# Three weight chunk halves get slots of their own in SBUF, and one goes back to the ring

## The chip, the cores and the metric

The kernel runs on one core of one Trainium2 chip. The metric is the device time of one execution in microseconds; before the change it is 531.22 us, the median of three runs (530.62 to 531.57). The names of the engines: PE is TensorE (PEld its weight loads), DVE is VectorE, ACT is ScalarE, POOL is GpSimd, and SP is the queue from which the loads are issued.

## The reference

One layer of a decoder trunk on 256 positions and 1024 features. Cut to what matters, the products that the change touches are these:

```python
h = rms_norm(x, norm_mix_g)
u_conv, q, kc, vc, ks, vs, kw, vw, g_nsa_heads, g_conv, g_attn = split(h @ w_in)
conv_out = silu(layer_norm(depthwise_conv(a * sigmoid(gt)) + b)) @ conv_pw_w
nsa_out  = nsa_attention(q, kc, vc, ks, vs, kw, vw, g_nsa_heads)
y = sigmoid(g_conv) * conv_out + sigmoid(g_attn) * nsa_out
x = x + y @ w_out
x = x + cross_attention(rms_norm(x, norm_x_g), mem)
x = x + swiglu(rms_norm(x, norm_ffn_g))
out = rms_norm(x, final_norm_g)
```

q is 1024 columns of `w_in`, `g_attn` 1024 more, and `conv_pw_w` is 1024 by 1024; everything is float32.

## The kernel before

**Chunks.** All weights are cut into chunks of 256 output columns, in the order in which they are used: k0 to k3 (cross-attention keys), u0 to u7 (the convolution's input), kc, vc, q0 to q3, ks, kw, vs, vw, ga0 to ga3 (the attention gate), gc0 to gc3 (the convolution's gate), pw0 to pw3, wo0 to wo3, xq0 to xq3, v0 to v3 (placed among the scores), xo0 to xo3, and the feed-forward chunks f. A chunk comes in two loads of 512 KB, each with four of the eight blocks of 128 input features. The two are called halves of a chunk here: q3_0 is the first half of the fourth q chunk, q3_1 its second.

**High and low.** To multiply float32 numbers with the faster type (fp32r), each operand is split into a high part (rounded by a copy) and a low part (the rest). `split` (L193) makes both for a chunk half: ACT copies the high part (L205), and a subtraction gives the low one (L208), on POOL for the chunks u3 to ga3 and on DVE for the others. Each product is then three: high by high, high weights by low activations, low weights by high activations. `rows` (L286) issues these for a chunk half, 24 matmuls (L297) of 128x128 weights on 256 moving columns: 16 with the high part of the weights, then 8 with the low part. In the profile a row `ps_q<-hh,q_0h` is such a matmul: the sum of a q chunk, moving operand hh (the high part of h; hl is the low one), weights the high part of a first half. The number of the chunk is left out in these names, but not that of the half.

**Where the halves lie.** Usually a high part takes one of five buffers of a ring (tag `whi`), and a low part one of five of a second ring (`wlo`). A chunk half named in `set_apart` (L217) lies elsewhere: with two tags, its high part begins 64 elements into the large slot of the first tag, and its low part 112 elements into the slot of the second. The large slots, L0 to L14, hold 8 KB for each partition and are shared by tiles that live at different times; LL is twice as large. The slots that the change names hold, one after the other:

- L9: `hf` (h as float32, read last by the gate logits, `g_ps`, L710), later `stacked`.
- L10 and L14: `kdh` and `kdl`, the keys of the scores, read until the last score product; later `yh` and `yl`.
- L11 and L13: in L13 `zins`, the input of the compression MLP; later `sga` and `sgc`, the two gates.

In the kernel's layout the start of a moving operand stands 448 bytes, modulo 512, behind the start of the weights that follow when those lie in a ring. For a high part set apart it is 256, and for a low part set apart 64.

**What sets the order.** Each engine works through its own queue in order, and the order of each queue is set when the kernel is built, by a scheduler that takes what becomes ready first by its own estimate. TensorE's order from kc on is held besides by `in_line`. A tile of a pool can be written when the last reader of the tile that lay there before is done, so where a half lies also sets what its copy has to wait for, and so where the copy stands in ACT's, DVE's or POOL's queue. The products run in the order of the chunks, with score products, transposes and outputs of the attention put between the chunks from ga0 on; pw0 to pw3 (L1040), wo and xq0 follow each other without anything between.

Of the kernel before, what the change touches and what calls it, by code (L numbers as in the profile page):

```python
# [118 lines left out]
def tile_hybrid_block(  # L119
# [97 lines left out]
    def set_apart(name, tag, low=None):  # L217

        pair = []

        def hi():
            pair.append(sb.tile([P, 1024 + 64 if low else 2 * 1024 + 112], F32R, tag=tag, name=f"{name}h"))
            return pair[0][:, 0:1024 + 64]

        def lo():
            if low:
                return sb.tile([P, 1024 + 112], F32R, tag=low, name=f"{name}l")[:, 112:]
            return pair[0][:, 1024 + 112:]

        apart[name], aparts[name] = hi, lo  # L230
# [2 lines left out]
    set_apart("xq1_0", "LL")  # L233
    set_apart("xq2_0", "LL")
    set_apart("xo0_1", "LL")
    set_apart("ks_0", "L11", "L13")
    set_apart("f2_0", "L9", "L0")

    def behind(*marks):
# [1314 lines left out]
```

## The time and the profile before

| | |
|---|---|
| three timed runs | 530.62, 531.22, 531.57 us |
| profiled execution, its own time | 528.97 us |
| span of it | 527.2 us |
| TensorE busy | 520.1 us, 4319 instructions |
| DVE, ACT, POOL busy | 442.3, 368.4, 147.4 us |
| granted clock of TensorE, mean | 0.997 |

The profile covers the profiled execution, which has a time of its own beside its span; the timed runs were made without it. In a timeline a row stands for several like instructions: its start, how long they took together, the engine, the line, the operation, `out<-in`, the shapes, and their number. Matmuls overlap, so the time that one adds is read from the distance of two starts and not from its own duration. A grouped row ends with the busy time, the mean duration of one in ns, and the idle time before. A window's row gives its length and then the busy time of PE, PEld, DVE, ACT and POOL, each with a count, the granted clock, the share of the DMA engines and GB/s.

### The profile page before, as it was taken

To read this page: it belongs to the slowest core of one execution; us is meant where nothing else is said; L and a number is where in the kernel's file an instruction comes from. 1 tells how busy PE (TensorE), PEld (TensorE's weight loads), DVE (VectorE), ACT (ScalarE), POOL (GpSimd) and SP (SyncE) were. 2 spreads that over 40 slices of the span, in tenths; PEclk is the share of its full clock that TensorE was granted. 3 is DMA by queue.
4 is the path that set the end of the run, shared out by engine and by line. 5 is a ranking of instruction groups with operands and counts; after the bars stand their busy time and mean duration, and the time that the engine had idled before them with its cause. 6 is when DMAs were issued, how large, how long until landed. Compare 5 with 4: busy or idle time off the path is not lost.

```text
span 527.2 us, 11194 instructions
## 1 busy us (share of the span) xinstructions
PE 520.1 (99%) x4319; PEld 502.4 (95%) x4319; DVE 442.3 (84%) x861; ACT 368.4 (70%) x671; POOL 147.4 (28%) x105
## 2 busy tenths in 40 slices
PE   9999999999999999999999999999999999999995
PEld 8999999999899999999999999999999999988884
DVE  4887899999999999984969685688988786689996
ACT  5678784999967899789648675565665555557743
POOL 0019889999995000330004000310000000000002
PEclk9999999999999999999999999999999999999998
DMA  8947966544545436224667542368665665625402
GB/s 315 410 168 250 322 202 212 165 161 153 166 160 184 160 127 208 88 81 160 222 217 274 192 156 99 109 197 300 229 219 192 197 201 188 201 93 159 162 0 81
DMA packets 29445, 97.20 MB, mean 184 GB/s; under 512 B 3152, under 2 KB 5456, under 8 KB 29136
## 3 DMA queue, kind: packets, MB, share of 16 engines
q1 hardware_dynamic: 28816, 95.44, 53.9%
q10 hardware_dynamic: 576, 1.05, 0.5%
q8 instruction: 34, 0.56, 0.4%
q14 instruction: 19, 0.16, 0.1%
HBM read 95.23 MB, written 1.25 MB: 183 GB/s over the span
## 4 chain that ended last, share of the span: by engine, by line
PE 98%; DVE 1%; ACT 0%; issue 0%; ACTq 0%
PE ps_f L297 23%; PE ps_u L297 8%; PE fo L1313 6%; PE ps_v L297 4%; PE ps_gc L297 4%; PE ps_ga L297 4%; PE ps_q L297 4%; PE ps_xq L297 4%; PE ps_pw L297 4%; PE ps_wo L297 4%; PE fos L1313 4%; PE ps_k L297 3%; PE ps_xo L297 3%; PE ps_xo L1198 2%; PE o L920 1%; PE s L852 1%
## 5 line engine op out<-in xcount | busy, mean ns | idle before, releaser
L494 DVE SCALAR_TENSOR_TENSOR yp<-vt,ppt,yp 128x256 f32<-128x256 f32 x144 | 64.2, 485 | 6.3 <-ACT yp L486 4.6
L1382 POOL TENSOR_TENSOR x<-xs,gf 128x512 f32<-128x512 f32 x2 | 2.6, 1302 | 168.3 <-issue 168.3
L297 PE MATMUL ps_f<-g,f_1h 128*128 128x256 f32 x352 | 44.4, 277 | 0.0
L297 PE MATMUL ps_f<-g,f_0h 128*128 128x256 f32 x352 | 43.9, 277 | 0.0
L297 PEld LDWEIGHTS ps_f<-g,f_1h 128*128 128x128 f32 x352 | 41.9, 188 | 0.0
L297 PEld LDWEIGHTS ps_f<-g,f_0h 128*128 128x128 f32 x352 | 41.8, 188 | 0.0
L205 ACT ACTIVATE f_0h<-f 128x1024 fp32r<-128x1024 f32 x22 | 23.4, 1062 | 18.9 <-issue 15.5
L886 ACT ACTIVATE p<-p,mins 128x128 f32<-128x128 f32 (+1 forms) x64 | 28.3, 449 | 10.2 <-DVE mins L865 10.0
L208 DVE TENSOR_TENSOR f_1l<-f,f_1h 128x1024 fp32r<-128x1024 f32 x22 | 27.4, 1247 | 5.6 <-ACT f_1h L205 5.6
L208 DVE TENSOR_TENSOR f_0l<-f,f_0h 128x1024 fp32r<-128x1024 f32 x22 | 27.3, 1243 | 3.2 <-ACT oxh L346 2.2
L205 ACT ACTIVATE f_1h<-f 128x1024 fp32r<-128x1024 f32 x22 | 23.2, 1060 | 9.4 <-PE ps_f L297 7.9
L486 ACT ACTIVATE vw<-vt,ppt 128x256 f32<-128x256 f32 x60 | 26.6, 499 | 0.6 <-DVE yp L508 0.5
L1272 DVE TENSOR_TENSOR ab<-ps_f,rf 128x512 f32<-128x512 f32 x22 | 15.2, 689 | 11.6 <-PE ps_f L297 11.6
L297 PE MATMUL ps_f<-g,f_1l 128*128 128x256 f32 x176 | 23.6, 277 | 0.0
L297 PE MATMUL ps_f<-g,f_0l 128*128 128x256 f32 x176 | 23.6, 276 | 0.0
L208 POOL TENSOR_TENSOR u_0l<-u,u_0h 128x1024 fp32r<-128x1024 f32 x5 | 12.0, 2404 | 37.5 <-ACT u_0h L205 37.5
L297 PEld LDWEIGHTS ps_f<-g,f_1l 128*128 128x128 f32 x176 | 21.7, 188 | 0.0
L297 PEld LDWEIGHTS ps_f<-g,f_0l 128*128 128x128 f32 x176 | 21.6, 188 | 0.0
L530 POOL TENSOR_TENSOR yt<-yt,vw 128x512 f32<-128x512 f32 x15 | 20.5, 1367 | 0.1
L508 DVE TENSOR_TENSOR yp<-yp,vw 128x512 f32<-128x512 f32 x28 | 19.4, 695 | 0.7
L748 POOL TENSOR_TENSOR ssum<-ssum,sq 128x512 f32<-128x512 f32 x3 | 4.7, 1580 | 44.9 <-ACT sq L747 44.7
L1274 ACT ACTIVATE sl<-ab 128x256 f32<-128x256 f32 x22 | 9.1, 417 | 11.0 <-DVE ab L1272 10.9
(845 smaller groups left out, 1667.4 us busy)
## 6 DMA issues: line engine op xcount, KB each, us to landing
f<-in_wst_dram SPq DMA_DIRECT2D x44, 512.0 KB, 4.4
u<-in_wst_dram SPq DMA_DIRECT2D x14, 512.0 KB, 6.9
for<-in_wfo_dram SPq DMA_DIRECT2D x14, 512.0 KB, 3.8
q<-in_wst_dram SPq DMA_DIRECT2D x8, 512.0 KB, 4.9
ga<-in_wst_dram SPq DMA_DIRECT2D x8, 512.0 KB, 3.3
gc<-in_wst_dram SPq DMA_DIRECT2D x8, 512.0 KB, 3.8
v<-in_wst_dram SPq DMA_DIRECT2D x8, 512.0 KB, 3.1
pw<-in_wst_dram SPq DMA_DIRECT2D x8, 512.0 KB, 4.6
```

The source lines that it names most:

```text
L205: copies = [nc.scalar.activation(hi[:, at:at + n], w[:, at:at + n], AF.Copy) for at in range(0, shape[1], n)]
L208: low = eng.tensor_tensor(out=lo[:, at:at + n], in0=w[:, at:at + n], in1=f(hi[:, at:at + n]), op=ALU.subtract)
L297: mm = nc.tensor.matmul(ps[:, b], lhsT=lhsT, rhs=rhs, start=row + b + kb == 0, stop=kb == NB - 1 and row == 2 and b == 1)
L486: nc.scalar.activation(to[:, i], vt[j + i][:, t:t + S], AF.Identity, scale=col(PP_DW + TAPS * (j + i), t), bias=col(PP_DB, j + i) if t == ...
L494: nc.vector.scalar_tensor_tensor(out=to[:, i], in0=vt[j + i][:, t:t + S], scalar=col(PP_DW + TAPS * (j + i), t), in1=acc[:, i], op0=ALU.mu ...
L508: nc.vector.tensor_tensor(out=to, in0=acc, in1=pr, op=ALU.add)
L530: nc.gpsimd.tensor_tensor(out=y, in0=y, in1=pr, op=ALU.add)
L886: exp.append(nc.scalar.activation(t, t, AF.Exp, scale=-1.0, bias=mins[:, hd, qb, br:br + 1], accum_out=sums[:, hd, qb, br:br + 1]))
L1198: nc.tensor.matmul(qs[:, b], lhsT=parts[m, 1][wi][:, k, cs], rhs=x[xi][:, 4 + k], start=False, stop=k == 3 and row == 2 and b == 1)
L1272: nc.vector.tensor_tensor(out=ab, in0=ps, in1=rf.unsqueeze(1).to_broadcast([P, 2, S]), op=ALU.mult)
L1274: silu = nc.scalar.activation(sl, ab[:, 0], AF.Silu)
L1313: mm = nc.tensor.matmul(o[:, cs], lhsT=t[x], rhs=w[y][:, cs], start=start and n == 0, stop=stop and n == 2)
```

## The change

The half ks_0 is no longer set apart and takes buffers of the two rings. q3_0 is set apart in L11 and L13, where ks_0 was; ga3_0 in L13 and L9; pw0_1 in L10 and L14.

```diff
     set_apart("xq1_0", "LL")
     set_apart("xq2_0", "LL")
     set_apart("xo0_1", "LL")
-    set_apart("ks_0", "L11", "L13")
+    set_apart("q3_0", "L11", "L13")
+    set_apart("ga3_0", "L13", "L9")
+    set_apart("pw0_1", "L10", "L14")
     set_apart("f2_0", "L9", "L0")
```

The number of instructions on each engine stays the same, and so does TensorE's order. Buffers of the rings go round differently from q3 to ks, and from ga3 on, since a half that is set apart takes none. All line numbers behind the edit are larger by two in the changed kernel.

Three places of the other engines' queues move. On POOL, at the end of q (1529 is the first half of q3, 1559 its second; `yt` is a sum of the convolution), before:

```order
L208 TENSOR_TENSOR q_0l<-q_0_1427,q_0h 128x1024
L208 TENSOR_TENSOR q_1l<-q_1_1457,q_1h 128x1024
L208 TENSOR_TENSOR q_0l<-q_0_1529,q_0h 128x1024
L208 TENSOR_TENSOR ks_0l<-ks_1624,ks_0h 128x1024
L530 TENSOR_TENSOR yt<-yt,vw_2_1287 128x512
L208 TENSOR_TENSOR q_1l<-q_1_1559,q_1h 128x1024
```

and with the change:

```order
L208 TENSOR_TENSOR q_0l<-q_0_1427,q_0h 128x1024
L208 TENSOR_TENSOR q_1l<-q_1_1457,q_1h 128x1024
L208 TENSOR_TENSOR q_1l<-q_1_1559,q_1h 128x1024
L208 TENSOR_TENSOR q_0l<-q_0_1529,q_0h 128x1024
L532 TENSOR_TENSOR yt<-yt,vw_2_1287 128x512
L208 TENSOR_TENSOR ks_0l<-ks_1624,ks_0h 128x1024
```

The second half of q3 has come ahead of the first, and ks_0 stands behind a piece of the convolution.

On POOL, at the attention gate (2155 and 2185 are the halves of ga2, 2243 and 2273 those of ga3), before:

```order
L208 TENSOR_TENSOR ga_0l<-ga_0_2155,ga_0h 128x1024
L530 TENSOR_TENSOR yt<-yt,vw_11_1785 128x512
L208 TENSOR_TENSOR ga_1l<-ga_1_2185,ga_1h 128x1024
L208 TENSOR_TENSOR ga_0l<-ga_0_2243,ga_0h 128x1024
L530 TENSOR_TENSOR yt<-yt,vw_12_1863 128x512
L208 TENSOR_TENSOR ga_1l<-ga_1_2273,ga_1h 128x1024
```

and with the change:

```order
L208 TENSOR_TENSOR ga_0l<-ga_0_2155,ga_0h 128x1024
L208 TENSOR_TENSOR ga_0l<-ga_0_2243,ga_0h 128x1024
L532 TENSOR_TENSOR yt<-yt,vw_11_1785 128x512
L208 TENSOR_TENSOR ga_1l<-ga_1_2185,ga_1h 128x1024
L208 TENSOR_TENSOR ga_1l<-ga_1_2273,ga_1h 128x1024
L532 TENSOR_TENSOR yt<-yt,vw_12_1863 128x512
```

The first half of ga3 has come ahead of the second half of ga2.

On ACT, at the last softmax (`p_7`, `p_14`, `p_15` are its exponentials; 3523 is the second half of pw0, 3555 and 3585 the halves of pw1, 3617 the first half of pw2), before:

```order
L910 ACTIVATE ptt_a_3197<-pt_a_3192 128x512
L886 ACTIVATE p_7_3250,sums<-p_7_3250,mins 128x128 x4
L205 ACTIVATE pw_0h<-pw_0_3555 128x1024
L886 ACTIVATE p_14_3265,sums<-p_14_3265,mins 128x256 x2
```

and with the change:

```order
L912 ACTIVATE ptt_a_3197<-pt_a_3192 128x512
L205 ACTIVATE pw_1h<-pw_1_3523 128x1024
L888 ACTIVATE p_7_3250,sums<-p_7_3250,mins 128x128 x4
L205 ACTIVATE pw_1h<-pw_1_3585 128x1024
L888 ACTIVATE p_14_3265,sums<-p_14_3265,mins 128x256 x2
```

The copy of pw0_1, which stood four instructions ahead of this piece, now stands right in front of the exponentials, and pw1's second half has taken the place of its first between them. On SP the load of a second half of gc now stands ahead of two loads of bias rows, where it stood behind them.

## The prediction

> **What bounds the kernel now.** I read the page's busy times and clock row first, then the chain that ended last.
>
> ```profile
> PE 520.1 (99%) x4319; PEld 502.4 (95%) x4319; DVE 442.3 (84%) x861; ACT 368.4 (70%) x671; POOL 147.4 (28%) x105
> PEclk9999999999999999999999999999999999999998
> PE 98%; DVE 1%; ACT 0%; issue 0%; ACTq 0%
> ```
>
> TensorE is busy for 520.1 of 527.2 us, at its full clock in all slices but the last, and it is 98% of the chain. So time can come only from three places: fewer matmuls, a shorter interval between two matmuls, or a new wait in front of one. The change leaves the number of matmuls and TensorE's order as they are. What is left is the interval, and the waits.
>
> The second view is TensorE's timeline. Each row is eight matmuls (128x128 weights, 256 moving columns) with the start of the first, so the difference of two starts over the count is the interval. Here is the end of the fourth q chunk, then ks, whose first chunk half (ks_0) is set apart before the change:
>
> ```profile
> 104.25 1.19 PE L297 MATMUL ps_q<-hh,q_0h 128*128 128x256 f32 x8
> 105.27 1.10 PE L297 MATMUL ps_q<-hl,q_0h 128*128 128x256 f32 x8
> ...
> 109.98 1.12 PE L297 MATMUL ps_ks<-hh,ks_0h 128*128 128x256 f32 x8
> ...
> 111.90 1.07 PE L297 MATMUL ps_ks<-hh,ks_0l 128*128 128x256 f32 x8
> ...
> 115.53 1.07 PE L297 MATMUL ps_kw<-hh,kw_0h 128*128 128x256 f32 x8
> ```
>
> The 40 matmuls from 105.27 to 109.98 stand 117.8 ns apart, the 16 of ks_0h from 109.98 to 111.90 stand 120.0 apart, and the 32 from 111.90 to 115.53 stand 113.4 apart. Operation, shape and clock are the same in all three, and none waits. So there are three paces: 120.0 on a set-apart high half, 117.8 ("slow") and 113.4 ("fast") on halves in the ring. The grouped view has the same three as durations:
>
> ```profile
> L297 PE MATMUL ps_q<-hh,q_0l 128*128 128x256 f32 x8 | 1.1, 281 | 0.0
> L297 PE MATMUL ps_ks<-hh,ks_0h 128*128 128x256 f32 x8 | 1.1, 283 | 0.0
> L297 PE MATMUL ps_ks<-hh,ks_0l 128*128 128x256 f32 x8 | 1.1, 276 | 0.0
> ```
>
> 283 is the set-apart high half, 281 slow and 276 fast. What differs is where the operands lie. By the kernel's layout the moving operand starts 448 bytes after the next weights (modulo 512) when these lie in the ring, 256 when they are a set-apart high half, and 64 when a set-apart low half. My reading: at 448 the pace is one of two and stays as it is until something changes it; a set-apart chunk half pays 120.0 for 16 matmuls, and whatever pace stood before, it is fast behind it. The change moves such resets. Where slow stretches lie is seen in the next rows.
>
> ```profile
> 154.43 1.11 PE L297 MATMUL ps_ga<-hh,ga_0h 128*128 128x256 f32 x8
> 160.09 1.10 PE L297 MATMUL ps_gc<-hh,gc_0h 128*128 128x256 f32 x8
> 165.74 0.40 PE L852 MATMUL s<-kdh,qt 128*128 128x512 f32 x1
> 167.13 1.11 PE L297 MATMUL ps_gc<-hh,gc_0h 128*128 128x256 f32 x8
> 168.08 1.10 PE L297 MATMUL ps_gc<-hl,gc_0h 128*128 128x256 f32 x8
> ```
>
> ga3 and gc0, 48 matmuls each, take 5.66 and 5.65 us: 117.8, slow throughout. The score products that follow leave gc1 slow again (8 in 0.95 us), so a reset at ga3_0 is worth something up to 165.74 and no further.
>
> ```profile
> 241.26 3.61 PE L297 MATMUL ps_pw<-z,pw_0h 128*128 128x256 f32 x30
> 244.71 1.07 PE L297 MATMUL ps_pw<-z,pw_0l 128*128 128x256 f32 x8
> ...
> 263.07 1.07 PE L297 MATMUL ps_wo<-yh,wo_0h 128*128 128x256 f32 x8
> ...
> 284.83 1.07 PE L297 MATMUL ps_xq<-gh,xq_0h 128*128 128x256 f32 x8
> ...
> 287.55 1.12 PE L297 MATMUL ps_xq<-gh,xq_0h 128*128 128x256 f32 x8
> ```
>
> The first 30 of pw average 115.0, a mixture; after that pw and wo run fast (192 of wo in 21.76 us, 113.3) until xq1_0, which is set apart, at 287.55. In this execution pw0_1 has nothing to reset.
>
> **The change part by part.** The sum is made against the profiled execution, 528.97 us with 527.2 of span; the three timed runs (530.62 to 531.57, median 531.22) all lie 1.6 to 2.6 us above it. That difference decides the case, as the third part shows.
>
> q3_0 and ks_0: q3_0h goes from 117.8 to 120.0, 16 x 2.2 ns = +0.035 us. The 32 behind it in q3 go from 117.8 to 113.4, -0.141. ks_0h returns to the ring and goes from 120.0 to 113.4, 16 x 6.6 = -0.106. Behind it nothing changes. Together -0.21 us.
>
> ga3_0: +0.035 for its own high half, -0.141 for the 32 behind it in ga3, and 48 x 4.4 ns = -0.211 for gc0. Together -0.32 us.
>
> pw0_1: there are two answers, by the pace that stands in front of it. If it is fast, as profiled, the 16 of its high half cost 6.6 ns more each: +0.106 us. If it is slow in the timed runs, its high half costs +0.035, and the 8 of its low half, 144 left of pw, 192 of wo and 24 of xq0_0 gain 4.4 each: 368 x 4.4 = -1.62, net -1.58 us. Which one holds in runs without a profile no trace shows. For slow speaks that such a stage entered slow and not recovered costs about 390 x 4.4 = 1.7 us, and 528.97 + 1.7 = 530.7 is what the lowest timed run shows; the one longer fast stretch, the feed-forward part, has a reset of its own at its start (f2_0). And how pw became fast looks like chance: it began slow and turned during the first 30. I take slow, and keep both ends.
>
> Copies and subtractions on other engines: none is added, but they move, because a half that has its own slot waits for that slot's last reader instead of for the ring. On POOL, whose order in the q and ga stages is shown ahead of this text:
>
> ```profile
> 92.31 2.41 POOL L208 TENSOR_TENSOR q_0l<-q,q_0h 128x1024 fp32r<-128x1024 f32 x1
> 95.82 2.46 POOL L208 TENSOR_TENSOR ks_0l<-ks,ks_0h 128x1024 fp32r<-128x1024 f32 x1 [1.10 <-ACT ks_0h L205]
> ...
> 143.28 2.45 POOL L208 TENSOR_TENSOR ga_1l<-ga,ga_1h 128x1024 fp32r<-128x1024 f32 x1
> 145.65 2.44 POOL L208 TENSOR_TENSOR ga_0l<-ga,ga_0h 128x1024 fp32r<-128x1024 f32 x1
> ...
> 106.21 1.11 PE L297 MATMUL ps_q<-hh,q_0l 128*128 128x256 f32 x8
> 152.13 1.07 PE L297 MATMUL ps_ga<-hh,ga_1l 128*128 128x256 f32 x8
> ```
>
> q3_0l ends about 2.4 us later, near 97, and TensorE reads it at 106.21; ks_0l ends near 101 against 111.90. The low half of ga2_1 falls behind that of ga3_0 and ends near 148.1 instead of 145.7; TensorE reads it at 152.13, so 4.0 us of cover are left. On SP one load of gc overtakes two bias loads, which ask for 1.24 us from 162.01 and are first read at 168.64. These I cost at nothing.
>
> The tight place is the last softmax, on ACT and DVE:
>
> ```profile
> 162.01 1.24 SPq L601 DMA_DIRECT2D nb<-line  x2
> 168.64 0.28 DVE L865 CUSTOM_DVE_ANT_0 p<-s,nb 128x128 f32<-128x128 f32 x1
> ...
> 223.62 0.40 PE L852 MATMUL s<-kdl,qt 128*128 128x512 f32 x1
> 224.74 0.40 ACT L886 ACTIVATE p<-p,mins 128x128 f32<-128x128 f32 x1 [1.05 <-DVE mins L865]
> 226.30 1.04 ACT L205 ACTIVATE pw_0h<-pw 128x1024 fp32r<-128x1024 f32 x1
> 232.11 0.28 DVE L896 TENSOR_SCALAR p<-p,sums 128x128 f32<-128x128 f32 x1
> 232.56 0.60 PE L907 MATMUL pt_b<-cpt,p 128*128 128x128 f32 x4
> ```
>
> pw0_1's slots were read last by the score product that ends at 224.02, so its 1.05 us copy now stands on ACT between there and the first exponential: 225.1 instead of 224.74, 0.36 us late. The copy that stood at 226.30 is replaced by another of the same length, so the lateness stays until the last scaling, 232.75 instead of 232.39, and the transposes that TensorE starts at 232.56 (weights from 232.45) come 0.2 to 0.36 late. Bounds: 0, if some of the 0.36 is absorbed on ACT, to 0.36; I take 0.3, since DVE's scaling ends just ahead of the transposes.
>
> Sum if pw was slow: -0.21 - 0.32 - 1.58 + 0.3 = -1.81 us. If pw was fast: -0.21 - 0.32 + 0.11 + 0.3 = -0.12 us.
>
> The Trainium skill speaks against any of this: in TensorE: Matmul & The Clock Gate, section "Step-by-step: what each phase is for", TensorE has two independent read ports on SBUF, one for the moving operand and one for the weights, so that loading the next weights takes no bandwidth from the running matmul; SBUF — State Buffer, section "SBUF: two separate sides", adds that TensorE never waits on anyone there. By that the place of the halves would be worth nothing. The trace disagrees: 276, 281 and 283 ns for one shape at one clock.
>
> **The rivals.** (1) Pw runs fast in the timed runs too, as in the profile. Time: 531.22 - 0.12 = 531.1. For it: the one execution that can be looked into. Against it: the 1.6 to 2.6 us that the timed runs are longer.
>
> (2) The place does nothing: the three paces go with the stage and not with the distance, so ks_0h in the ring stays at 120 and ga3 at 117.8. Then only the softmax is left, 531.22 + 0.3 = 531.5. Against it stands that 120.0 begins at 109.98 and ends at 111.90, exactly with the tile.
>
> (3) Slower, by one mechanism: POOL, which issues in order, is held at the moved low half of ga3_0, because its slot (the ninth large one, read by the gate logits) or its high half on ACT comes free late, and with it ga2_1 and ga3_1 behind it. It decides from the point where ga2_1's low half is over 4.0 us late. POOL has no gap there:
>
> ```profile
> 104.00:120.00 16.00, 16.00 (x140) 16.00 (x140) 15.65 (x36) 14.76 (x32) 16.00 (x11) 1.00 0.48 157
> 120.00:154.00 34.00, 34.00 (x313) 32.04 (x313) 32.79 (x59) 32.73 (x62) 33.92 (x20) 1.00 0.46 152
> ```
>
> POOL (fifth figure) is busy in 33.92 of 34 us there, so time lost isn't regained. Another 2.44 for a half in front and a delay as long would make 7 us, that is 3 us of waiting: 531.1 + 3 = 534. With the pw gain it would be 532.4. Against it: the gate logits' matmuls, which read that slot last, end long ahead of 142, where the moved piece would start:
>
> ```profile
> 132.64 1.25 PE L710 MATMUL g_ps<-hf,wg 128*64 128x256 f32 x10
> ```
>
> **How the numbers follow.** Pw slow in the timed runs 0.48, pw fast 0.34, no effect of the place 0.05, POOL late or a like wait 0.13. A measurement of this kernel tells about 0.2%, 1.06 us, from no change. The forecast -1.81 is faster by that bound with about nine chances in ten, since the stretches that enter fast by chance are drawn anew (0.2 to 0.5 us each); with small shares of the other cases faster is 0.45. Same takes rivals (1) and (2) and the rest of the forecast, 0.42; slower 0.13. The predicted time is 531.22 - 1.81 = 529.4. Its own range is 528.8 to 530.2. For 8 in 10 it has to reach over rival (1) and (2): 528.7 to 531.8. Below lies a further lucky entry, above it rival (3).
>
> **What would show it.** In the timeline of the changed kernel q3_0h, ga3_0h and pw0_1h at 120.0 ns apart, what follows them at 113.4, ks_0h no longer at 120.0, gc1 slow again after its scores: the reading is right. If the profiled execution of the changed kernel is only some tenths under 528.97 while its timed runs come down by 1.8, the timed runs of before were slow in pw and wo; if both stand still, rival (1) holds. A stretch that stays at 117.8 behind a set-apart half breaks the rule of resets. Transposes that wait for DVE near 232 show the softmax term, an idle TensorE near 148 to 156 rival (3).

## The result, and the profile after

The change makes the kernel slower. Its median is 533.76 us (531.37 to 535.28), that of the kernel before 531.29 (529.26 to 533.06), each of 10 runs; the ratio is 1.0053, 95% interval 1.0034 to 1.0073. Forecast were 529.4 us and a range of 528.7 to 531.8, so the forecast was wrong in its sign, and the range did not hold the time. The profiled execution of the change took 534.78 us (span 533.0) against 528.97 (527.2) before, 5.8 more. That is over twice the difference of the medians, because the execution profiled before lies below all ten of its kernel's runs, and this one near the upper end of its own.

The page of the changed kernel, busy times and chain that ended last:

```profile
PE 521.8 (98%) x4319; PEld 502.6 (94%) x4319; DVE 442.9 (83%) x861; ACT 368.9 (69%) x671; POOL 148.1 (28%) x105
PE 78%; DVE 13%; ACT 3%; issue 2%; DMA 2%; POOL 1%; DVEq 0%; ACTq 0%; POOLq 0%
```

Busy times hardly moved, but TensorE's share of the chain fell from 98% to 78%: there are waits now that are ended by DVE and by what DVE is held by. The view of TensorE's waits in the changed kernel lists them (in total, how often, the longest, in us):

```profile
PE ps_gc L299 <- ACT sga L765: 1.5, 1, 1.5
PE cs_ps L795 <- ACT ct L786: 1.1, 1, 1.1
PE warm L408 <- DVE eps_t L180: 1.1, 1, 1.1
PE sp_l L399 <- POOL nr_l L371: 0.7, 1, 0.7
PE ct_ps L782 <- DVE kdl L697: 0.4, 1, 0.4
PE pt_b L909 <- DVE mins L867: 0.4, 1, 0.4
```

In the same view of the kernel before stands one row only:

```profile
PE warm L406 <- DVE eps_t L180: 1.1, 1, 1.1
```

The other five add 4.1 us, of the 5.8. The longest, ahead of gc0, is for `sga`, ACT's copy of a finished gate sum. In the changed kernel's timelines that copy stands on ACT behind a piece of the convolution (`vw`), which waits 4.73 us for a sum on DVE (`yp`), and that sum stands on DVE behind the subtractions of gc0_0 (4.84) and gc0_1 (2.24); DVE, then ACT:

```profile
151.58 4.84 DVE L208 TENSOR_TENSOR gc_0l<-gc,gc_0h 128x1024 fp32r<-128x1024 f32 x1
...
159.94 0.69 DVE L510 TENSOR_TENSOR yp<-yp,vw 128x512 f32<-128x512 f32 x1
...
160.72 1.71 ACT L530 ACTIVATE vw<-vt,ppt 128x256 f32<-128x256 f32 x4 [4.73 <-DVE yp L510]
```

The experiments take this chain apart. The paces are read from TensorE's timeline of the changed kernel:

```profile
106.64 1.07 PE L299 MATMUL ps_q<-hh,q_0l 128*128 128x256 f32 x8
...
110.27 1.07 PE L299 MATMUL ps_ks<-hh,ks_0h 128*128 128x256 f32 x8
...
112.08 1.07 PE L299 MATMUL ps_ks<-hh,ks_0l 128*128 128x256 f32 x8
...
143.11 0.66 PE L795 MATMUL cs_ps<-cpt,ct 128*128 128x128 f32 x4 [1.06 <-ACT ct L786]
143.96 1.19 PE L299 MATMUL ps_ga<-hh,ga_0h 128*128 128x256 f32 x8
144.99 1.11 PE L299 MATMUL ps_ga<-hl,ga_0h 128*128 128x256 f32 x8
145.93 1.10 PE L299 MATMUL ps_ga<-hh,ga_0l 128*128 128x256 f32 x8
...
157.70 1.12 PE L299 MATMUL ps_ga<-hl,ga_0h 128*128 128x256 f32 x8
158.66 1.07 PE L299 MATMUL ps_ga<-hh,ga_0l 128*128 128x256 f32 x8
...
161.38 1.07 PE L299 MATMUL ps_ga<-hh,ga_1l 128*128 128x256 f32 x8
163.91 1.21 PE L299 MATMUL ps_gc<-hh,gc_0h 128*128 128x256 f32 x8 [1.46 <-ACT sga L765]
164.96 1.10 PE L299 MATMUL ps_gc<-hl,gc_0h 128*128 128x256 f32 x8
165.90 1.10 PE L299 MATMUL ps_gc<-hh,gc_0l 128*128 128x256 f32 x8
```

Where the halves were put, the paces are those forecast. The 32 matmuls behind q3_0h, from 106.64 to 110.27, stand 113.4 ns apart; ks_0h, back in the ring, takes 16 x 113.1 (110.27 to 112.08); the last eight of ga3_0h take 120.0 each (157.70 to 158.66), and the 24 behind them 113.3. But the pace can be another one behind a wait. Behind the wait at 143.11, ga1 goes at 117.5 (144.99 to 145.93), where before it went at 113; behind the wait at 163.91, gc0 goes at 117.5, so the reset at ga3_0 brings nothing there in this execution.

The starts of the same rows before and after place the loss: +0.3 us at the first ks row (109.98 to 110.27), +3.8 at the first gc row (160.09 to 163.91), +5.75 at sp_l, the last norm's small matmuls (232.12 to 237.87), and only 0.1 more behind that. The 0.3 is no loss at q: +0.41 is there from the first k chunk on (11.02 to 11.43), ahead of everything that the change touches, and at the first kw row +0.18 is left, so that q gains 0.23. Between ks and gc lie waits of 0.4, 1.1 and 1.5, and ga1 and ga2 at the slow pace, about 96 x 4.4 ns = 0.4. Between gc and sp_l lie waits of 0.4 and 0.7. By the starts the transposes cost more than the waits listed for them: 0.3 at 175.14 and 0.5 at 184.96.

### The profile page after: what moved, and what is told of

The parts are those of the page before. It is cut to its first block, busy times and chain, and to the rows that moved or that the text cites. A ratio compares the mean times of both kernels' runs of the same rounds, so it can differ in the third digit from the quotient of the medians.

```text
span 533.0 us, 11194 instructions
## 1 busy us (share of the span) xinstructions
PE 521.8 (98%) x4319; PEld 502.6 (94%) x4319; DVE 442.9 (83%) x861; ACT 368.9 (69%) x671; POOL 148.1 (28%) x105
## 4 chain that ended last, share of the span: by engine, by line
PE 78%; DVE 13%; ACT 3%; issue 2%; DMA 2%; POOL 1%; DVEq 0%; ACTq 0%; POOLq 0%
PE ps_f L299 23%; PE ps_u L299 8%; PE fo L1315 6%; DVE yp L496 4%; PE ps_xq L299 4%; PE ps_pw L299 4%; PE ps_wo L299 4%; PE ps_v L299 4%; PE fos L1315 4%; PE ps_k L299 3%; PE ps_xo L299 3%; DMA q<-in_wst_dram 2%; PE ps_xo L1200 2%; DVE yp L510 1%; DVE gc_1l L208 1%
```

## The experiments

Where an expectation speaks of theory A, it is that the loss comes from the copy of q3_1 on ACT, which waits for its load ahead of the copies of q's sums. Theory R is that it comes from the ring: a half that is set apart takes no ring buffer, so the halves behind it get theirs one place earlier, and their copies and subtractions come earlier in ACT's and DVE's queues, ahead of work that is more urgent. Theory B is rival 3 of the prediction, the order of POOL's queue at the gate, and theory C its softmax term, the last softmax held by the copy of pw0_1. Ratios are to the kernel before, run beside each, with a 95% interval; they can differ a little from the quotient of two medians.

### One part at a time

**q alone** (q3_0 apart, ks_0 not):

```diff
-    set_apart("ks_0", "L11", "L13")
+    set_apart("q3_0", "L11", "L13")
```

> Only the q edit: q3_0 is set apart where ks_0 was; ga3_0 and pw0_1 stay in the rings. Theory A (the copy of q3_1's high part now stands on ScalarE ahead of the copies of q0's sums, waits there for its load, and VectorE's convolution is held behind those): the whole loss is here, 2 to 3 us slower than before, and VectorE sits idle for some us near 94 with ScalarE as the releaser. Theory B (the moved low half of ga3_0 on POOL): nothing is lost, about -0.2 us. Theory C (the last softmax, held by the copy of pw0_1): nothing is lost either, -0.2 us.

Measured: 531.71 us, ratio 1.0012 (0.9992 to 1.0032): no difference that can be told. There is a new hole on DVE, though, in its timeline of this run:

```profile
95.98 0.42 DVE L674 SCALAR_TENSOR_TENSOR qt<-ps_q,qt 64x256 fp32r<-64x256 f32 x1 [2.97 <-ACT qt L672]
```

It is there in the changed kernel too (3.84), whose ACT timeline shows why. The copy of q3's second half waits for its load, and the copies of q0's sums (qt), for which DVE waits, stand behind it:

```profile
95.45 1.06 ACT L205 ACTIVATE q_1h<-q 128x1024 fp32r<-128x1024 f32 x1 [1.07 <-DMA q<-in_wst_dram]
96.41 0.36 ACT L673 ACTIVATE qt<-ps_q 64x256 fp32r<-64x256 f32 x1
```

So DVE loses 3 to 4 us near 96. In this run the view lists no wait of TensorE for that (its one new wait is 0.4 at pt_b). But between the first ct_ps and the first gc row TensorE still slips by 0.66 us against before: 0.20 at cs_ps (141.10), and the rest in ga1 and ga2, which run at 117.8 behind it. Pw and wo ran at the slow pace in this profile, which is taken up below.

**The gate and pw, without q** (ks_0 stays apart):

```diff
     set_apart("ks_0", "L11", "L13")
+    set_apart("ga3_0", "L13", "L9")
+    set_apart("pw0_1", "L10", "L14")
```

> ks_0 stays set apart as before, ga3_0 and pw0_1 are set apart as in the change. Theory A: no loss of some us; -0.3 us at the gate, and at pw between +0.4 and -1.3 us, so a ratio of 0.997 to 1.000. Theory B: 2 to 3 us slower, with TensorE idle near 141 and 162. Theory C: 0.3 to 1 us slower, with an idle TensorE only behind 232.

Measured: 534.38 us, ratio 1.0061 (1.0040 to 1.0082), from six runs. The whole loss is there without the edit at q. TensorE waits 1.7 us ahead of gc0, 1.6 for the minima ahead of two transposes, and 0.7 at sp_l.

**pw alone**:

```diff
     set_apart("ks_0", "L11", "L13")
+    set_apart("pw0_1", "L10", "L14")
```

> Only pw0_1 is set apart in addition to before. If pw and wo run slow in the timed runs of before: 1.3 us faster (ratio 0.9975). If they run fast: +0.1 us for the high half at 120 ns and up to +0.3 from the late softmax (ratio 1.0002 to 1.0008). Theory C in its strong form: more than 0.5 us slower.

Measured: 531.25 us, ratio 1.0018 (1.0002 to 1.0035). The gain of 1.6 that the forecast took from here is missing, and a small loss stands in its place (0.02 to 0.35%). Most of the loss of the run before is therefore the gate's: 1.0061 against 1.0018.

**The change with q3_1's copy behind the compression sigmoid**, which takes away the hole near 96:

```diff
-        nc.scalar.activation(zs, z_ps, AF.Sigmoid)
+        first["q3_1"] = nc.scalar.activation(zs, z_ps, AF.Sigmoid),
```

> The change with all three halves set apart, but the copy of q3_1's high part is made to wait for the sigmoid of the compression MLP on ScalarE, so that it stands behind the copies of q0's sums, about where it stood before. Theory A: the loss of the change goes away, 0 to 2 us faster than before (ratio 0.996 to 1.000), and TensorE no longer waits near 141 and 162. Theories B and C: as slow as the change, ratio 1.005.

Measured: 534.42 us, ratio 1.0077 (1.0052 to 1.0101). Theory A falls as an explanation of the loss. The profiled execution was the fastest of the twelve (531.97) and has no wait at ct_ps and cs_ps; those ahead of gc0 (0.8), at sp_l (0.7) and at pt_b (0.4) are still there.

### The gate: POOL's order or the ring

**ga3_0 apart, with POOL's order as before.** The mark holds ga3_0's copy back until the low half of ga2_1 has been issued, so that on POOL it no longer overtakes:

```diff
     def split(w, shape, name):
...
+        if name == "ga3_0":
+            first[name] = splits["ga2_1"]
...
     set_apart("ks_0", "L11", "L13")
+    set_apart("ga3_0", "L13", "L9")
```

> Only ga3_0 is set apart in addition to before, and its copies wait for those of ga2_1, which gives POOL its old order back; the halves of gc still move one place ahead on ScalarE and VectorE, because the rings have a buffer more. If the moved low half on POOL makes the loss (theory B as first put): same as before, -0.3 us, no wait of TensorE ahead of gc0. If it is the gc halves on VectorE (theory R: gc0_0's subtraction, held by POOL for 4 to 7 us, now stands ahead of a convolution sum that ScalarE waits for, and ScalarE's copy of ga2's sum stands behind that): TensorE still waits 1 to 2 us ahead of gc0, and the time is 1.5 to 2.5 us above before (ratio 1.003 to 1.005).

Measured: 533.95 us, ratio 1.0042 (1.0019 to 1.0066). With POOL's order restored the loss stays, so rival 3's mechanism is not what sets it. What holds TensorE ahead of gc0 is seen in the timeline of this run, DVE, then POOL, ACT and TensorE:

```profile
149.21 6.89 DVE L210 TENSOR_TENSOR gc_0l<-gc,gc_0h 128x1024 fp32r<-128x1024 f32 x1
156.03 1.53 DVE L497 SCALAR_TENSOR_TENSOR yp<-vt,ppt,yp 128x256 f32<-128x256 f32 x3
157.59 0.70 DVE L511 TENSOR_TENSOR yp<-yp,vw 128x512 f32<-128x512 f32 x1
...
150.13 1.29 POOL L533 TENSOR_TENSOR yt<-yt,vw 128x512 f32<-128x512 f32 x1
151.38 2.39 POOL L210 TENSOR_TENSOR ga_1l<-ga,ga_1h 128x1024 fp32r<-128x1024 f32 x1
153.73 1.29 POOL L533 TENSOR_TENSOR yt<-yt,vw 128x512 f32<-128x512 f32 x1
155.10 2.15 POOL L727 TENSOR_TENSOR ysum<-yt 128x512 f32<-128x512 f32 x1
...
158.38 0.91 ACT L531 ACTIVATE vw<-vt,ppt 128x256 f32<-128x256 f32 x2 [4.93 <-DVE yp L511]
161.78 0.58 ACT L766 ACTIVATE sga<-ps_ga 128x512 f32<-128x512 f32 x1
...
162.41 1.19 PE L300 MATMUL ps_gc<-hh,gc_0h 128*128 128x256 f32 x8 [1.51 <-ACT sga L766]
163.44 1.07 PE L300 MATMUL ps_gc<-hl,gc_0h 128*128 128x256 f32 x8
164.35 1.07 PE L300 MATMUL ps_gc<-hh,gc_0l 128*128 128x256 f32 x8
```

Read it from the end. TensorE waits 1.51 us ahead of gc0 for `sga`, the copy by which ACT empties the PSUM bank of ga2's sum. On ACT that copy stands behind a piece of the convolution (`vw`, L531) that has waited 4.93 us for a sum on DVE (`yp`, L511); between the two on ACT are two copies of gc halves, which wait 0.3 and 0.2 us for their loads. On DVE that sum stands behind gc0_0's subtraction, which takes 6.89 us. Alone the same instruction takes about 1.2 (rows `pw_1l` below). It starts while POOL works without a gap, and ends 1.1 us after POOL's first gap (155.02 to 155.10): POOL's next instruction then takes 2.15. Behind this wait, as long as the one in the changed kernel, gc0 goes fast (163.44 to 164.35, 113.8 each).

The late DVE costs more than that one wait. The softmax, whose pieces lie in the gc stage, begins on DVE with the minima (`mins`, L868). Their first instruction starts at 165.93, 3.5 us behind the first matmul of gc0; in the kernel before it starts at 159.69, 0.4 us ahead of it. Two transposes behind the minima wait 1.4 and 0.4 us (pt_b in the view of TensorE's waits), more in sum than gc0 does.

In the kernel before, the same subtraction is held too, but the sum stands ahead of it in DVE's timeline:

```profile
148.87 0.70 DVE L508 TENSOR_TENSOR yp<-yp,vw 128x512 f32<-128x512 f32 x1
149.48 4.57 DVE L208 TENSOR_TENSOR gc_0l<-gc,gc_0h 128x1024 fp32r<-128x1024 f32 x1
```

There its 4.57 us cost nothing: TensorE has no wait. The Trainium skill, SBUF — State Buffer, section "SBUF: two separate sides", has VectorE and GpSimd share a port pair that is an exclusive lock for a whole instruction, where VectorE reads two operands from SBUF and GpSimd reads SBUF. The rows agree, 6.89 us against 1.2, and show more: the lock was not had at the change from one POOL instruction to the next, but only at a gap. In all thirteen profiles this subtraction ends 1.08 to 1.09 us after POOL's first gap behind its start.

**ga3_0 apart, with gc0_0 behind the convolution sum** (that of tap 27, for which ACT waits), and gc1_1 behind the first minima:

```diff
+    added = {}
...
-                nc.vector.tensor_tensor(out=to, in0=acc, in1=pr, op=ALU.add)
+                added[j, t] = nc.vector.tensor_tensor(out=to, in0=acc, in1=pr, op=ALU.add)
...
+    first["gc0_0"] = added[4, 27],
...
+    first["gc1_1"] = mins_of[0],
```

> Only ga3_0 is set apart in addition to before, POOL keeps the moved order, but the copies of gc0_0 wait for the convolution sum (tap 27) that stood ahead of them before, and those of gc1_1 for the first minima. Theory R: the wait ahead of gc0 and the one of the first transposes go away, and the resets' gain is left: -0.3 us, ratio 0.998 to 1.001. Theory B: still 1.5 us or more slower, with the wait ahead of gc0.

Measured: 531.02 us, ratio 0.9994 (0.9969 to 1.0019). The loss of 2.3 us (533.95 against 531.67 before) is gone, with two marks that change nothing but the order of copies and subtractions. POOL keeps the moved order here, so the run differs from the one above in that as well; the pair that differs in marks alone follows below, with pw0_1 apart in both. In the timeline of this run, DVE and ACT:

```profile
153.43 0.70 DVE L511 TENSOR_TENSOR yp<-yp,vw 128x512 f32<-128x512 f32 x1
154.03 4.36 DVE L208 TENSOR_TENSOR gc_0l<-gc,gc_0h 128x1024 fp32r<-128x1024 f32 x1
...
154.60 1.69 ACT L531 ACTIVATE vw<-vt,ppt 128x256 f32<-128x256 f32 x4
```

The sum is ahead again, ACT's piece no longer waits for it, and the wait ahead of gc0 is 0.2 instead of 1.5. The first minima start 0.7 us behind gc0's first matmul instead of 3.5, and 0.4 of the 1.8 us at the transposes is left. The subtraction still takes 4.36. Theory R holds for the gate; which of the two marks brings how much was not measured. (This profiled execution, 532.63, has two waits that belong to the compression, in the view of TensorE's waits; the loads of q were issued late in it, and the edit does not touch them.)

```profile
PE ct_ps L784 <- DVE kdl L698: 1.2, 1, 1.2
PE cs_ps L797 <- ACT ct L788: 0.7, 1, 0.7
```

### Pw: the norm's steps on POOL, and the pace

**pw0_1 apart, with pw1_1 behind a late copy of the transposed exponentials (ACT, L911):**

```diff
     set_apart("ks_0", "L11", "L13")
+    set_apart("pw0_1", "L10", "L14")
...
+    first["pw1_1"] = copies[-4],
```

> Only pw0_1 is set apart in addition to before, and the copies of pw1_1 wait for a later transposed copy, so that VectorE no longer does two subtractions of halves back to back at the last softmax. If these two hold POOL's Newton steps for the last norm and so TensorE (about 0.8 us at the matmuls that spread the norm): that wait shrinks to under 0.3 us, and the time falls by about 0.8 us against the run with pw0_1 alone (ratio to before 0.998 to 1.001 instead of 1.0018). If the scaling of the softmax holds TensorE, as the prediction had it: the wait stays.

Measured: 529.89 us, ratio 0.9983 (0.9956 to 1.0010), against 1.0018 (1.0002 to 1.0035) without the mark. In the run without it (pw alone), the timelines of DVE, POOL and TensorE show two subtractions back to back, pw0_1 and pw1_1, and under them two steps of the last norm's Newton iteration on POOL:

```profile
227.54 2.36 DVE L208 TENSOR_TENSOR pw_1l<-pw,pw_1h 128x1024 fp32r<-128x1024 f32 x2
...
227.29 0.20 POOL L368 TENSOR_TENSOR nt_l<-nt_l,r_l 128x2 f32<-128x2 f32 x1
227.58 1.23 POOL L369 TENSOR_SCALAR nt_l<-nt_l 128x2 f32<-128x2 f32 x1
228.89 1.06 POOL L370 TENSOR_TENSOR nr_l<-nr_l,nt_l 128x2 f32<-128x2 f32 x1
...
233.84 0.71 PE L398 MATMUL sp_l<-cpt,nr_l 128*128 128x128 f32 x4 [0.72 <-POOL nr_l L370]
```

With the mark only one subtraction is left there, one step is held, and TensorE does not wait at sp_l; the same timelines of that run:

```profile
227.31 1.22 DVE L208 TENSOR_TENSOR pw_1l<-pw,pw_1h 128x1024 fp32r<-128x1024 f32 x1
...
227.35 1.23 POOL L369 TENSOR_SCALAR nt_l<-nt_l 128x2 f32<-128x2 f32 x1
228.66 0.20 POOL L370 TENSOR_TENSOR nr_l<-nr_l,nt_l 128x2 f32<-128x2 f32 x1
...
232.80 0.71 PE L398 MATMUL sp_l<-cpt,nr_l 128*128 128x128 f32 x4
```

A step that takes 0.20 alone took 1.23 and 1.06. So the wait at sp_l comes from pw1_1, which the freed ring buffer let come earlier: in the four profiles with pw0_1 apart and no mark on pw1_1 it is 0.7 us, and in the five with the mark it is not there. The times alone (two overlapping intervals) don't settle its size. Nor do the spans, 529.1 without the mark and 528.0 with it: the two executions are already 1.1 us apart in the first k chunk, and the one with the mark waits 0.7 at two transposes.

**The pace of pw and wo** can be compared over all profiles. In two of the runs without pw0_1 apart, q alone and ga3_0 with POOL's order, they entered slow, and the grouped row of wo has 281 ns; q alone:

```profile
L297 PE MATMUL ps_wo<-yh,wo_0h 128*128 128x256 f32 x32 | 4.4, 281 | 0.0
```

In the kernel before and in the run with gc0_0 behind the sum, also without pw0_1 apart, the row has 276. In all nine profiles with pw0_1 apart it has 276, as in pw alone:

```profile
L298 PE MATMUL ps_wo<-yh,wo_0h 128*128 128x256 f32 x32 | 4.3, 276 | 0.0
```

The rule of resets held nine times out of nine, and without a reset the slow pace came in two of four. The 1.6 us that the reset is worth in a slow execution is thus earned in some executions only, about half by these four, an estimate from few.

### The change and its parts, mended

**The gate and pw with the three marks** (gc0_0, gc1_1, pw1_1), ks_0 left apart:

```diff
     set_apart("ks_0", "L11", "L13")
+    set_apart("ga3_0", "L13", "L9")
+    set_apart("pw0_1", "L10", "L14")
...
+    first["gc0_0"] = added[4, 27],
...
+    first["gc1_1"] = mins_of[0],
...
+    first["pw1_1"] = copies[-4],
```

> ks_0, ga3_0 and pw0_1 set apart, with the three waits of the two runs before this one in the list (gc0_0, gc1_1, pw1_1). If the order on VectorE is the whole loss: -0.3 us at the gate and +0.1 to -1.6 us at pw, ratio 0.996 to 1.000. If a reset in itself costs something else: slower than before.

Measured: 529.99 us, ratio 0.9977 (0.9956 to 0.9998), against 1.0061 (1.0040 to 1.0082) without the marks. This pair differs in the marks alone, and POOL has the moved order in both. In this run's view of TensorE's waits only the one at the start is left (`warm`, 1.1).

**The whole change with the three marks:**

```diff
-    set_apart("ks_0", "L11", "L13")
+    set_apart("q3_0", "L11", "L13")
+    set_apart("ga3_0", "L13", "L9")
+    set_apart("pw0_1", "L10", "L14")
...
+    first["gc0_0"] = added[4, 27],
...
+    first["gc1_1"] = mins_of[0],
...
+    first["pw1_1"] = copies[-4],
```

> The whole change, q edit included, with the three waits of the mended run (gc0_0 behind the convolution sum of tap 27, gc1_1 behind the first minima, pw1_1 late); q3_1's copy stays ahead of the copies of q0's sums. If the q edit costs what the run with it alone showed (0.5 us, not clear of noise, VectorE idle 2 to 3 us near 94): ratio about 0.998 to 1.000. If the loss at the gate comes back because the convolution is later by the time it gets there: 1.002 to 1.004, with TensorE waiting near 141 to 163.

Measured: 531.07 us, ratio 0.9997 (0.9977 to 1.0017). The loss of 0.53% is gone, and its interval lies below that of the change. Waits of 0.5 at pt_b and 0.4 at cs_ps are left, and DVE's hole near 96 (2.43 us). No wait stands ahead of gc0, and the fast pace is kept there, as TensorE's timeline of this run shows:

```profile
161.52 1.07 PE L299 MATMUL ps_gc<-hh,gc_0h 128*128 128x256 f32 x8
162.43 1.07 PE L299 MATMUL ps_gc<-hl,gc_0h 128*128 128x256 f32 x8
```

Eight matmuls of gc0 take 0.91 us, 113.8 each, as forecast for the change itself.

**The same with q3_1 late too:**

```diff
-        nc.scalar.activation(zs, z_ps, AF.Sigmoid)
+        first["q3_1"] = nc.scalar.activation(zs, z_ps, AF.Sigmoid),
```

> The same, and q3_1's copy waits for the sigmoid of the compression MLP, as in the earlier run. If VectorE's idle time at q is what the q edit costs: 0.3 to 1 us faster than the run before this one, and as fast as or 0.2 us faster than the mended run without the q edit (ratio 0.996 to 0.998). If the q edit costs something by the moved halves of ks to vw on POOL: slower than the mended run without it.

Measured: 530.49 us, ratio 0.9991 (0.9973 to 1.0009). The 0.6 us under the run before go the way of a small cost of q3_1's copy, but the intervals overlap almost wholly.

**The mended gate and pw once more**, the same edits as above, to see whether the gain of 0.23% is real:

> The mended version without the q edit once more, unchanged: ratio 0.9956 to 0.9998 as before if that was more than chance; and its profile shows how much of TensorE's waits differ from one execution to the next.

Measured: 530.56 us, ratio 0.9988 (0.9967 to 1.0008). The first gain is not confirmed. Its profile has a wait of 0.4 at pt_b that the first one did not have, so waits of that size come and go between executions of one kernel. The mended version is 0.1 to 0.2% under the kernel before in both, and whether it is faster stays open.

What none of these runs settles is the spread: the kernel before alone went from 529.26 to 533.06 in its ten runs. Profiles of different kernels differ in the pace of pw and wo, which is worth 1.6 us, in when the loads of q are issued, and in the first k chunk, whose rows lie from 0.3 us ahead of those in the profile of before to 1.0 us behind them; what decides these in one execution was not found.

## Why the prediction was wrong

**Right: what bounds the kernel, and the three paces.** TensorE's order and work stayed as they were, and set-apart high halves at 120.0, 113.3 to 113.4 behind them, ks_0h down from 120.0, and gc1 slow again behind its scores all came as worked out, so rival (2) falls. The terms for q (-0.21, measured -0.23) and for ga3 itself were right. That for gc0 (-0.21) was not had in the changed kernel, where gc0 went slow behind its wait; it was had in the mended change, and in the run with POOL's order even behind a wait of 1.51.

**The step that failed is "These I cost at nothing".** It followed the halves that were set apart, and asked whether each is ready when TensorE reads it. All were. What it did not follow are the halves behind them in the ring, gc0_0, gc1_1 and pw1_1, which get their buffers one place earlier because a set-apart half takes none. Nobody waits for these early; what stands behind them on DVE is late. At the gate that is the convolution's sum, behind a subtraction that POOL holds for 4 to 7 us instead of 1.2, then ACT, a PSUM bank and TensorE: 0.8 to 1.7 us ahead of gc0 in the four profiles without marks, and 0.4 to 1.8 more at transposes, of which up to 0.7 comes in other kernels too. The cost of the step was 2.3 us by the median of ga3_0 alone with POOL's order as before. That the order is the cause is shown by the marks: 1.0061 becomes 0.9977, and the change's 1.0053 becomes 0.9997. The share of gc1_1 was not measured by itself. The row with 4.57 for a subtraction stood in the profile of before, and DVE's new order followed from the change; the prediction looked at POOL's, ACT's and SP's.

**Mis-sized: pw0_1, -1.58.** The reset works, but the text took the slow pace for all timed runs, since they lay 1.6 to 2.6 us above the profiled one. By four profiles without the reset it holds in about half: an estimate of -0.8 on average, not -1.58. Of that the wait at sp_l gave 0.7 back. What is left by this estimate, -0.1, is still a little under what pw alone measured (+0.1 to +1.9 us by its interval).

**Right place, wrong chain: the softmax term, +0.3.** A wait near 232 did come, but not by ACT's late exponentials and DVE's scaling. It is POOL's Newton steps under two of DVE's subtractions, and 0.7 us. In the kernel before, POOL's last step of the norm ends at 231.79 and TensorE needs it at 232.12, a cover of 0.3 us that the prediction did not look at.

**Rival (3) had the sign, and not the cause.** It put the loss at the gate, between 148 and 156, through POOL's queue, at 534 or 532.4; that the measured 533.76 is near is luck. But the run with POOL's order restored keeps the loss, and POOL was not late for TensorE: POOL held DVE. Its chance, 0.13, was too small because it was tied to that one mechanism.

**Left open.** The hole on DVE near 96 is shown; what it costs is not. In the changed kernel's profiled execution TensorE waited 0.4 and 1.1 us for the compression, and in the one with q alone it slipped by 0.66 there. But waits at the same places came in a run without the edit at q, and the two pairs of runs that differ in q3_1's copy alone point in opposite directions (1.0053 and 1.0077; 0.9997 and 0.9991).

## What to carry to other kernels

When a tile is taken out of a ring of buffers, look at the tiles that stay in it: each later one gets its buffer earlier, its producers move forward in every in-order queue, and the question is who stands behind them there. For every instruction that moves ahead on an engine, take its longest duration from the profile and not its shortest, since an instruction that is harmless at the end of a queue can be held for several us at another place. A gain of nanoseconds per instruction can be lost at every wait that enters the stretch.

## What the runs showed of the hardware

**DVE is kept out over several POOL instructions.** A subtraction of 128x1024 with both operands in SBUF, 1.2 us alone, took 4.57 (before), 4.84 (the change), 6.92 (the gate and pw) and 6.89 us (ga3_0 with POOL's order), depending on how long POOL went on without a gap from where it started. The other way round POOL got in between two subtractions of DVE: two steps of 0.2 us took 1.23 and 1.06, one for each subtraction.

**The pace is drawn at an entry, and a wait is an entry.** Ring halves of one shape at one clock ran at 113 or 118 ns, and mostly stayed so for a whole stage. Ga1 and ga2 went slow in all five profiles in which cs_ps, ahead of them, waited (0.04 to 1.06 us), and fast in the eight others. Behind a wait ahead of gc0 (six profiles, 0.1 to 1.7 us) gc0 went slow in two and fast in four. Wo was slow in two of four profiles without a reset and in none of nine with one. What the draw depends on is not known.
